# The delta rule's residual of four heads: one broadcast product and one addition in place of four fused operations

## The chip, the cores and the metric

The kernel runs on one core of a Trainium2 chip. The metric is the device time of one execution in microseconds (us): 2305.68 in the median of three runs, from 2304.61 to 2306.77.

A core has engines that work through queues of their own and wait for each other through semaphores: TensorE (PE in the profile; its weight loads are listed as PEld) multiplies matrices, VectorE (DVE), ScalarE (ACT) and GpSimd (POOL) work on tiles, SyncE (SP) issues the transfers. Each engine takes its queue in order: an instruction that waits holds up everything behind it on that engine. Matrix products are written to PSUM, which has eight banks; all else lies in SBUF.

## The reference

Two layers of a hybrid block: a Mamba-2 branch (SSD), latent attention (MLA) and a gated DeltaNet branch read one input projection; their outputs are gated, projected and followed by an MLP. Sequence 512, width 1024, everything in float32. The change lies in the DeltaNet branch, whose core is this (cut):

```python
    rhs = jnp.concatenate([v * beta[..., None], kb * jnp.exp(g)[..., None]], axis=-1)
    sol = lax.linalg.triangular_solve(a_mat + jnp.eye(L, dtype=jnp.float32), rhs,
                                      left_side=True, lower=True)
    u, w = jnp.split(sol, [DV], axis=-1)
...
    def step(state, inp):
        qc, kc, uc, wc, gc, ac = inp
        v_new = uc - jnp.einsum('bhld,bhdv->bhlv', wc, state)
        o = (jnp.einsum('bhld,bhdv->bhlv', qc * jnp.exp(gc)[..., None], state)
             + jnp.einsum('bhlm,bhmv->bhlv', ac, v_new))
        g_last = gc[..., -1:]
        state = (state * jnp.exp(g_last)[..., None]
                 + jnp.einsum('bhld,bhlv->bhdv', kc * jnp.exp(g_last - gc)[..., None], v_new))
        return state, o
...
    o = rmsnorm(o, norm_g) * jax.nn.silu(z.astype(jnp.float32).reshape(Bsz, S, GDN_V_HEADS, GDN_HEAD_V))
```

There are eight value heads of width 128 and four key heads of width 128, so that two value heads share a key head. The kernel puts the solve behind the state: it forms the residual r = v - decay * (k . state) of a chunk first and multiplies it with the inverse of the triangular matrix, which gives v_new.

## The kernel before

*Dense products.* A projection is made of fp32r products of 128x512. To keep float32's accuracy each weight and each activation is split into a high and a low half, and each product is three matmuls (L182, L183, L184). A weight is loaded by SP (L161, `wraw`, two buffers), cast to its high half on ACT (L154, `whi`) and subtracted on DVE (L155, `wlo`); of `whi` and `wlo` there are four buffers each, so a cast waits until PE has used the half from four casts before. The results go to four PSUM banks called `acc`. Everything else that PE writes goes to three banks `sm`, and transposed outputs to one bank `yt`.

*The DeltaNet part.* `gdn_unit(u, ...)` handles four value heads; it is called for u = 0 and u = 1 in each layer. It first makes queries (`key_tiles`, with norms L968, L970, L972), transposed keys (L977, copied at L978), values (projected and transposed at L988, scaled at L989) and gates. Then it loops over t = 0..3, chunks of 128 tokens:

- L1003 the product of keys and queries, L1005 masks it, L1007 multiplies it into the decays `e` (both its inputs are in SBUF);
- for t > 0: L1012 the product of keys and state into a bank `pk`, then L1014, four fused operations of 128x128, one a head: r = pk * ndec + r. `ndec` is a negative decay, one number for each token and head;
- L1017 multiplies r with the inverse, one product a head; L1019 scales the result to `vn` (tag `wk1`, one buffer), L1024 to `vd` on ACT;
- for t < 3: L1027 the state's update, L1030 (t = 0) or L1033 the new state;
- L1036 and L1041 the two parts of the output, L1042 the copy of the first on ACT (L1046 at t = 0), L1044 adds the second;
- the norm of the output: L1050 squares on ACT with sums, L1056 and L1057 scale the sums, then `rsq`: L258 on DVE and L259, a power, on POOL; L1059 finishes it and L1062 multiplies norm, output and gate, one operation a head.

After the loop L1067 transposes the gated outputs, sixteen of 128x128 in a unit, into `yt`, and L254 and L255 split them into halves. So the norm of chunk t-1 (L1050 to L1062) runs beside the recurrence of chunk t, on the same queues.

*What sets the order.* The program is written in the order above, but the order of each engine's queue comes from a scheduler with priorities, at build time. It fills PE with dense products of other projections: beside u = 0 those for the queries, values and gates of u = 1, beside u = 1 those of the gate inputs and of the output projection. It also pulls single transpositions L1067 up into the loop, and puts casts L154 and splits L155 between the recurrence's work on ACT and DVE. The numbers at the end of tile names below tell buffers apart.

Of the kernel before, what the change touches and what calls it, by code (L numbers as in the profile page):

```python
# [10 lines left out]
F32 = mybir.dt.float32  # L11
# [4 lines left out]
ALU = mybir.AluOpType  # L16
# [4 lines left out]
P = 128  # L21
# [34 lines left out]
def hybrid_kernel(ctx, tc, a, out, depth=2, taps=None):  # L56
    nc = tc.nc
    pe, act, dve, pool, sync = nc.tensor, nc.scalar, nc.vector, nc.gpsimd, nc.sync
    uid = itertools.count()

    def mk(pl, shape, dt, tag, bufs=None):
        return pl.tile(shape, dt, tag=tag, name=f"{tag}_{next(uid)}", bufs=bufs)
# [12 lines left out]
    def bc_last(ap, n):  # L75
        sh = list(ap.shape)
        return ap.unsqueeze(len(sh)).to_broadcast(sh + [n])
# [15 lines left out]
    def sm_bank():  # L93
        return mk(ps_sm, [P, 512], F32, "sm")
# [256 lines left out]
    for ly in range(depth):  # L351
# [198 lines left out]
        for hp in range(4):  # L550
# [121 lines left out]
            if hp == 0:  # L672
                dec, ndec, beta, dtq, dsk = step_sizes()
# [25 lines left out]
        br = bp.enter_context(tc.tile_pool(name="br", bufs=1, reuse_waits="tile"))  # L699
# [102 lines left out]
        hv = lambda x: x.rearrange("p (h n) -> p h n", h=4)  # L802
# [157 lines left out]
        def gdn_unit(u, kT, ork, cc, cd, Yt, yh, yl):  # L960
# [20 lines left out]
            for i in range(2):  # L981
                for j, pj in enumerate(dense_F(weights(w_in, O_GV + (4 * u + 2 * i) * P, 256, D), tiles(256), D, xh, xl)):
                    h = 2 * i + j
# [12 lines left out]
            for t in range(T):  # L996
# [11 lines left out]
                r = v[:, t, :]  # L1008
                if t > 0:
                    pk = sm_bank()  # L1010
                    for i in range(2):
                        pe.matmul(pk[:, i * 256 : (i + 1) * 256], kT[i][:, tok], st[:, i * 256 : (i + 1) * 256], start=True, stop=True)  # L1012
                    for h in range(4):
                        dve.scalar_tensor_tensor(hv(r)[:, h], hv(pk)[:, h], ndec[:, t, 4 * u + h : 4 * u + h + 1], hv(r)[:, h], ALU.mult, ALU.add)  # L1014
                pw = sm_bank()
                for h in range(4):
                    pe.matmul(pw[:, h * P : (h + 1) * P], Y[:, h, :], r[:, h * P : (h + 1) * P], start=True, stop=True)  # L1017
# [77 lines left out]
        for u in range(2):  # L1095
            gdn_unit(u, *mats[u], *yg)
# [97 lines left out]
        with tc.tile_pool(name="wo", bufs=1, reuse_waits="tile") as wo:  # L1194
# [8 lines left out]
            h = mk(hpl, [P, T, D], F32, "h")  # L1203
# [204 lines left out]
```

## Time and profile before

| what | value |
|---|---|
| median of 3 runs | 2305.68 us (2304.61 to 2306.77) |
| the profiled execution | 2304.96 us |
| its span, first to last instruction | 2303.2 us |
| mean clock granted to PE | 0.998 of full speed |
| PE / PEld / DVE / ACT / POOL busy | 98 / 81 / 71 / 52 / 3% of the span |
| window 585 to 664 us (units 0 and part of 1, layer 1) | PE busy 78.10 of 79.00 us, DVE 58.32 |
| window 676 to 714 us (unit 1's loop, layer 1) | PE busy 35.70 of 38.00 us, DVE 24.31 |

All numbers but the first line come from one profiled execution. A row of a group gives line, engine, operation, output and inputs, how many, busy us and mean ns, then the idle time before them and what ended it. A row of the chain of waits gives start, duration and what the end of the program was waiting for at that moment. A row of the timeline gives start, duration, engine, line and operation, and in brackets the idle time before and its releaser. Layer 1's units run at about 585 to 720 us, layer 2's at the same distance from its own start.

### The profile page before, as it was taken

To read this page: it belongs to the slowest core of one execution; us is meant where nothing else is said; L and a number is where in the kernel's file an instruction comes from. 1 tells how busy PE (TensorE), PEld (TensorE's weight loads), DVE (VectorE), ACT (ScalarE), POOL (GpSimd) and SP (SyncE) were. 2 spreads that over 40 slices of the span, in tenths; PEclk is the share of its full clock that TensorE was granted. 3 is DMA by queue.
4 is the path that set the end of the run, shared out by engine and by line. 5 is a ranking of instruction groups with operands and counts; after the bars stand their busy time and mean duration, and the time that the engine had idled before them with its cause. 6 is when DMAs were issued, how large, how long until landed. Compare 5 with 4: busy or idle time off the path is not lost.

```text
span 2303.2 us, 32278 instructions
## 1 busy us (share of the span) xinstructions
PE 2268.3 (98%) x11810; PEld 1864.5 (81%) x11810; DVE 1646.7 (71%) x3256; ACT 1201.6 (52%) x2509; POOL 59.4 (3%) x74
## 2 busy tenths in 40 slices
PE   8999999999999999999999999999999999999998
PEld 7888787888887888888888887878888877888886
DVE  7777566876666778767867775668757667778668
ACT  6766644333443465554657666443334435645545
POOL 0000000000000000000000000000000000000000
PEclk9999999999999999999999999999999999999999
DMA  4223633452324243233132236335422241433231
GB/s 142 80 74 101 192 101 112 130 144 74 87 69 158 71 147 102 92 102 116 49 102 79 74 108 194 97 111 146 120 82 83 65 164 55 156 110 101 92 110 46
DMA packets 220032, 244.16 MB, mean 106 GB/s; under 512 B 34256, under 2 KB 172384, under 8 KB 219872
## 3 DMA queue, kind: packets, MB, share of 16 engines
q1 hardware_dynamic: 219872, 242.09, 34.5%
q8 instruction: 93, 1.52, 0.3%
q14 instruction: 67, 0.55, 0.1%
HBM read 225.60 MB, written 11.74 MB: 103 GB/s over the span
## 4 chain that ended last, share of the span: by engine, by line
PE 91%; DVE 4%; ACT 2%; POOL 1%; DMA 1%; issue 1%; SPq 0%; DVEq 0%; POOLq 0%; ACTq 0%
PE acc L182 23%; PE acc L183 23%; PE acc L184 23%; PE sm L184 3%; PE sm L182 3%; PE sm L183 3%; DVE wlo L155 1%; PE sm L752 1%; PE sm L650 1%; ACT whi L154 1%; PE sm L1036 1%; POOL gms L259 1%; PE yt L666 1%; PE sm L290 1%; PE sm L630 1%
## 5 line engine op out<-in xcount | busy, mean ns | idle before, releaser
L155 DVE TENSOR_TENSOR wlo<-wraw,whi 128x512 fp32r<-128x512 f32 (+1 forms) x536 | 365.8, 687 | 345.1 <-ACT whi L154 338.4
L154 ACT CAST whi<-wraw 128x512 fp32r<-128x512 f32 (+1 forms) x536 | 329.5, 618 | 538.6 <-PE acc L183 366.8
L184 PE MATMUL acc<-xh,wlo 128*128 128x512 f32 (+1 forms) x1344 | 522.8, 389 | 0.0
L182 PE MATMUL acc<-xh,whi 128*128 128x512 f32 (+1 forms) x1344 | 522.7, 389 | 0.0
L183 PE MATMUL acc<-xl,whi 128*128 128x512 f32 (+1 forms) x1344 | 521.7, 388 | 0.0
L183 PEld LDWEIGHTS acc<-xl,whi 128*128 128x128 f32 x1344 | 253.0, 188 | 47.9 <-DVE xl L255 0.7
L182 PEld LDWEIGHTS acc<-xh,whi 128*128 128x128 f32 x1344 | 252.8, 188 | 47.9 <-ACT xh L254 0.4
L184 PEld LDWEIGHTS acc<-xh,wlo 128*128 128x128 f32 x1344 | 252.9, 188 | 47.5
L154 ACT CAST whi<-wr 128x512 fp32r<-128x512 f32 x168 | 104.2, 620 | 108.1 <-PE acc L183 47.8
L183 PE MATMUL acc<-yl,whi 128*128 128x512 f32 x384 | 151.5, 395 | 0.0
L182 PE MATMUL acc<-yh,whi 128*128 128x512 f32 x384 | 150.9, 396 | 0.0
L184 PE MATMUL acc<-yh,wlo 128*128 128x512 f32 x384 | 150.0, 391 | 0.0
L155 DVE TENSOR_TENSOR wlo<-wr,whi 128x512 fp32r<-128x512 f32 x168 | 113.5, 689 | 35.6 <-ACT whi L154 34.8
L691 DVE SCALAR_TENSOR_TENSOR ckl<-acc,pc,ckl 128x511 f32<-128x511 f32 (+2 forms) x168 | 120.4, 744 | 18.1 <-ACT ckl L687 10.8
L182 PEld LDWEIGHTS acc<-yh,whi 128*128 128x128 f32 x384 | 71.7, 188 | 15.9 <-ACT yh L254 1.7
L184 PEld LDWEIGHTS acc<-yh,wlo 128*128 128x128 f32 x384 | 72.2, 188 | 14.5
L183 PEld LDWEIGHTS acc<-yl,whi 128*128 128x128 f32 x384 | 72.2, 188 | 13.8
L183 PE MATMUL acc<-wlo,xh 128*128 128x512 f32 (+1 forms) x208 | 80.1, 385 | 0.0
L182 PE MATMUL acc<-whi,xh 128*128 128x512 f32 (+1 forms) x208 | 79.6, 384 | 0.0
L184 PE MATMUL acc<-whi,xl 128*128 128x512 f32 (+1 forms) x208 | 79.5, 384 | 0.0
L1148 DVE TENSOR_TENSOR h<-h,acc 128x512 f32<-128x512 f32 x120 | 77.1, 682 | 0.1
L454 ACT ACTIVATE eE<-eE,cum 128x128 f32<-128x128 f32 x192 | 63.2, 391 | 25.0 <-DMA eE<-d_c 23.3
(453 smaller groups left out, 4553.3 us busy)
## 6 DMA issues: line engine op xcount, KB each, us to landing
wraw<-in_w_in_dram SPq DMA_DIRECT2D x144, 512.0 KB, 3.7
wraw<-in_w_up_dram SPq DMA_DIRECT2D x64, 512.0 KB, 3.6
wr<-in_w_down_dram SPq DMA_DIRECT2D x32, 1024.0 KB, 5.2
eE<-d_c SPq DMA_DIRECT2D x48, 256.0 KB, 3.9
wraw<-in_w_mla_out_dram SPq DMA_DIRECT2D x16, 512.0 KB, 3.4
eE<-d_e SPq DMA_DIRECT2D x32, 256.0 KB, 2.7
wraw<-in_w_ssd_out_dram SPq DMA_DIRECT2D x16, 512.0 KB, 3.4
wraw<-in_w_gdn_out_dram SPq DMA_DIRECT2D x16, 512.0 KB, 3.3
```

Source lines behind the costliest of these rows:

```text
L154: act.copy(hi, raw)
L155: dve.tensor_tensor(lo, raw, f32(hi), ALU.subtract)
L182: pe.matmul(o, ah, bh, start=start, stop=False, skip_group_check=more)
L183: pe.matmul(o, ah, bl, start=False, stop=False, skip_group_check=more)
L184: pe.matmul(o, al, bh, start=False, stop=stop, skip_group_check=more)
L259: pool.tensor_tensor(o, o, (exp if exp is not None else nhalf)[:, : o.shape[1]], ALU.pow)
L290: pe.transpose(ps[:, j * P : (j + 1) * P], xr[j % 2][:, kk * P : (kk + 1) * P], ident)
L454: act.activation(o[:, i], o[:, i], AF.Relu, scale=-1.0, bias=cum[:, t, h0 + i : h0 + i + 1])
L630: pe.matmul(o, qps[j][:, tok], kps[:, :n], start=False, stop=False)
L650: pe.transpose(ps[:, n : n + P], pn[t][:, kb * P : (kb + 1) * P], ident)
L691: dve.scalar_tensor_tensor(acc[:, d:], ps[:, : S - d], taps_[3 - d], acc[:, d:], ALU.mult, ALU.add)
L1148: dve.tensor_tensor(hs_, hs_, ps[t], op)
```

## The change

The four operations of L1014 become two over all four heads. A new tile `kd_` takes the product of `pk` and `ndec`, where `ndec`'s four numbers a token are spread over 128 columns each by a broadcast access; a second operation adds it to r. `kd_` is of the tag `wk1`, so it takes the one buffer in which `vn` lies.

```diff
                         pe.matmul(pk[:, i * 256 : (i + 1) * 256], kT[i][:, tok], st[:, i * 256 : (i + 1) * 256], start=True, stop=True)
-                    for h in range(4):
-                        dve.scalar_tensor_tensor(hv(r)[:, h], hv(pk)[:, h], ndec[:, t, 4 * u + h : 4 * u + h + 1], hv(r)[:, h], ALU.mult, ALU.add)
+                    kd_ = mk(br, [P, 512], F32, "wk1")
+                    dve.tensor_tensor(hv(kd_), hv(pk), bc_last(ndec[:, t, 4 * u : 4 * u + 4], P), ALU.mult)
+                    dve.tensor_tensor(r, r, kd_, ALU.add)
                 pw = sm_bank()
```

It is one line longer, so what stood at L1017 stands at L1018 in the changed kernel, L1062 at L1063, and so on; the product is L1014 and the addition L1015. It acts at twelve places: two layers, two units, t = 1, 2, 3. 48 operations go and 24 come.

The scheduler makes other queues of it. On DVE at u = 0, t = 1 of layer 1 (`tok_5664` holds r, `tok_5665` the gates and outputs, `gms` the norm, `gk` and `eE` the masked products), from the first operation of the residual on, before:

```order
L1014 SCALAR_TENSOR_TENSOR tok_5664<-sm_6072,ndec_1105,tok_5664 128x128
L1005 TENSOR_TENSOR gk_6069<-sm_6066,ct_75 128x256
L1056 TENSOR_TENSOR gms_6054<-gos_6010,grt_6051 128x4
L1014 SCALAR_TENSOR_TENSOR tok_5664<-sm_6072,ndec_1105,tok_5664 128x128
L1057 TENSOR_TENSOR gms_6054<-gms_6054,grt_6051 128x4
L1007 TENSOR_TENSOR eE_6064<-eE_6064,gk_6069 128x512
L258 TENSOR_SCALAR gms_6054<-gms_6054 128x4
L1014 SCALAR_TENSOR_TENSOR tok_5664<-sm_6072,ndec_1105,tok_5664 128x128
L1059 SCALAR_TENSOR_TENSOR gms_6054<-gms_6054,grt_6051 128x4
L1014 SCALAR_TENSOR_TENSOR tok_5664<-sm_6072,ndec_1105,tok_5664 128x128
L1062 SCALAR_TENSOR_TENSOR tok_5665<-tok_5665,gms_6054,wk_1275_6041 128x128 x3
```

and in the changed kernel:

```order
L1014 TENSOR_TENSOR wk_1286_6075<-sm_6072,ndec_1105 128x512
L1057 TENSOR_TENSOR gms_6054<-gos_6010,grt_6051 128x4
L1005 TENSOR_TENSOR gk_6069<-sm_6066,ct_75 128x256
L1058 TENSOR_TENSOR gms_6054<-gms_6054,grt_6051 128x4
L1015 TENSOR_TENSOR tok_5664<-tok_5664,wk_1286_6075 128x512
L258 TENSOR_SCALAR gms_6054<-gms_6054 128x4
L1007 TENSOR_TENSOR eE_6064<-eE_6064,gk_6069 128x512
L1060 SCALAR_TENSOR_TENSOR gms_6054<-gms_6054,grt_6051 128x4
L1063 SCALAR_TENSOR_TENSOR tok_5665<-tok_5665,gms_6054,wk_1275_6041 128x128 x3
```

The fourth operation of the residual stood behind L1059, which takes POOL's result; now the whole residual stands ahead of L258, which feeds POOL. L1007 stood ahead of L258 and now stands behind it. At t = 2 and 3 the order is alike, with a split L155 behind the product at u = 1.

On PE at the same place, from the third dense product behind L1012 (`xh`, `xl` are halves of the input, `whi`, `wlo` of a weight) to the transposition; before:

```order
L1017 MATMUL sm_6079<-tok_5664,tok_4370 128x128
L183 MATMUL acc_6292<-xl_36_152,whi_6311 128x512
L184 MATMUL acc_6292<-xh_28_144,wlo_6312 128x512
L182 MATMUL acc_6292<-xh_29_145,whi_6311 128x512
L183 MATMUL acc_6292<-xl_37_153,whi_6311 128x512
L1017 MATMUL sm_6079<-tok_5664,tok_4370 128x128
L184 MATMUL acc_6292<-xh_29_145,wlo_6312 128x512
L1017 MATMUL sm_6079<-tok_5664,tok_4370 128x128
L1067 MATMUL yt_6261<-ct_75,tok_5665 128x128
```

and in the changed kernel:

```order
L183 MATMUL acc_6289<-xl_36_152,whi_6308 128x512
L184 MATMUL acc_6289<-xh_28_144,wlo_6309 128x512
L182 MATMUL acc_6289<-xh_29_145,whi_6308 128x512
L183 MATMUL acc_6289<-xl_37_153,whi_6308 128x512
L1018 MATMUL sm_6078<-tok_5664,tok_4370 128x128 x4
L184 MATMUL acc_6289<-xh_29_145,wlo_6309 128x512
L1068 MATMUL yt_6258<-ct_75,tok_5665 128x128
```

The four products with the inverse were spread between the dense ones, a head each; now they stand together, since all heads' residuals come at once. One dense product stands between the last of them and the transposition. How the counts of dense products (L182 to L184) changed at the other places of a layer, up to the product named:

| place | before | in the changed kernel |
|---|---|---|
| u0 t1, L1012 to the transposition, then to the state's update | 10, 11 | 10, 11 |
| u0 t2, L1012 to the state's update | 50: 8 among the four L1017, 7 up to the single L1067, then 35 with the other two L1017 among them | 41: 12 up to the four L1018, 28 up to the single L1068, 1 |
| u0 t3, L1012 to the output L1036 / L1037 | 50 | 23: 15 and 8 |
| u1 t1 | as u0 t1 | as u0 t1 |
| u1 t2, L1012 to the state's update | 26 | 24: 12, 1 up to L1068, 11 |
| u1 t3, L1012 to L1036 / L1037 | 19 | 21: 12, 1 up to L1068, 8 |

On ACT at the end of u0's loop (`whi_66..` are cast weights; `wk_1325` and `wk_1328` the output of t = 3), before:

```order
L154 CAST whi_6610<-wraw_6608 128x512
L154 CAST whi_6626<-wraw_6608 128x512
L154 CAST whi_6644<-wraw_6642 128x512
L1042 COPY wk_1325_6231<-sm_6226 128x512
L262 ACTIVATE ft_1376_6478<-ckl_1377_6479 128x512
L262 ACTIVATE ft_1379_6492<-ckl_1380_6493 128x512
L1050 ACTIVATE gk_6240,gos_6010<-wk_1325_6231 128x128
```

and in the changed kernel:

```order
L154 CAST whi_6557<-wraw_6539 128x512
L687 ACTIVATE ckl_1383_6490<-acc_6406,pc_121 128x512
L262 ACTIVATE ft_1379_6475<-ckl_1380_6476 128x512
L154 CAST whi_6607<-wraw_6605 128x512
L262 ACTIVATE ft_1382_6489<-ckl_1383_6490 128x512
L154 CAST whi_6623<-wraw_6605 128x512
L1043 COPY wk_1328_6228<-sm_6223 128x512
L978 COPY kt_6389<-sm_6391 128x512
```

The copy of the output stands one cast further up in the row of weights (two casts of the next pair ahead of it, where there were three), while its product L1037 moved 27 dense products further up. On PE behind that L1037 there now stand L1042, L968, 8 dense products, a single L1068, 14 dense products, L977, 2, L977, L988, 2, L988, 9 and the first L1068 of t = 3. No other queue changes but SP's, where the load of one chunk's `e` (L1000, u1 t3) stands ahead of two weight loads.

## The prediction

> **What bounds the kernel now.** I read the summary of engines and the chain of waits first, because they say which engine a saved microsecond must come from.
>
> ```profile
> span 2303.2 us, 32278 instructions
> PE 2268.3 (98%) x11810; PEld 1864.5 (81%) x11810; DVE 1646.7 (71%) x3256; ACT 1201.6 (52%) x2509; POOL 59.4 (3%) x74
> PE 91%; DVE 4%; ACT 2%; POOL 1%; DMA 1%; issue 1%; SPq 0%; DVEq 0%; POOLq 0%; ACTq 0%
> ```
>
> TensorE (PE) is busy 98% of the span, and 91% of the chain is PE. VectorE (DVE), whose instructions the change swaps, carries 4% of it. A shorter DVE helps only where PE stands still for it. So the second view is that of line L1014, the four operations to be replaced, with who waited for them; then the chain of waits around the first of its places, u = 0, t = 1 of layer 1.
>
> ```profile
> L1014 DVE SCALAR_TENSOR_TENSOR tok<-sm,ndec,tok x48: 342/347/354, 597.7 to 1844.9; 128x128 f32<-128x128 f32 x48
>   PEld sm L1017: 9.0, 22
> ...
> 590.38 0.89 PE sm L1017 x8
> ...
> 597.70 0.35 DVE tok L1014
> 598.05 0.39 DVE gk L1005
> 598.45 0.07 DVE gms L1056
> 598.52 0.26 DVE tok L1014
> 598.78 0.07 DVE gms L1057
> 598.85 0.60 DVE eE L1007
> 599.45 0.09 DVE gms L258
> 599.54 0.07 issue
> 599.61 1.02 POOL gms L259
> 600.65 0.16 DVE gms L1059
> 600.81 0.27 DVE tok L1014
> 601.13 0.49 PE sm L1017 x2
> ```
>
> 48 instructions stand for 12 places, 6 a layer. The waits on them come to 9.0 us in PE's weight loads, but the chain shows that the fourth L1014 is not late because DVE is slow: it stands in DVE's queue behind L1059, and L1059 waits 1.02 us for GpSimd's (POOL's) power L259, which belongs to the norm of the chunk before. PE waits for POOL through L1014. How PE's work goes on there is read in the timeline, together with a second place, u0 t2:
>
> ```profile
> 601.48 0.48 PE L182 MATMUL acc<-xh,whi 128*128 128x512 f32 x1
> 604.09 1.16 PE L1027 MATMUL sm<-wk,kt 128*128 128x256 f32 x4
> 610.02 0.69 DVE L1007 TENSOR_TENSOR eE<-eE,gk 128x512 f32<-128x512 f32 x1
> 610.20 1.38 POOL L259 TENSOR_TENSOR gms<-gms,nhalf 128x4 f32<-128x4 f32 x1 [9.59 <-DVE gms L258]
> 612.75 0.33 PE L1067 MATMUL yt<-ct,tok 128*128 128x128 f32 x1 [0.50 <-DVE tok L1062]
> 612.84 0.48 PE L184 MATMUL acc<-xh,wlo 128*128 128x512 f32 x1
> ```
>
> PE steps through dense products: between 601.48 and 604.09 there are 11, so 0.237 each, the first at about 0.31 and the others 0.23. At 601.13 and at 612.75 it waits. At the second place the one waiting is not L1017 but L1067, the transposition of a finished norm, and again for POOL.
>
> **The change, part by part.** *DVE's own work.* Four operations of 0.26 us from start to start (598.52 to 598.78 in the chain) make 1.04. The changed kernel has two of 128x512: a product of a PSUM tile with broadcast decays, and an addition of two SBUF tiles. Neither is in the trace at this place, but both kinds are elsewhere:
>
> ```profile
> L1019 DVE TENSOR_TENSOR wk<-sm,gcc 128x512 f32<-128x512 f32 x16 | 11.0, 688 | 3.0 <-PE sm L1017 3.0
> L763 DVE TENSOR_TENSOR tok<-tok,wk 128x512 f32<-128x512 f32 x12 | 8.2, 685 | 0.0
> ```
>
> L1019 is a PSUM product with a broadcast factor, L763 an addition within SBUF: 688 and 685 ns, in the chain 0.60 from start to start (L1007, which is as large). So 2 x 0.60 = 1.20 in place of 1.04: DVE issues 0.16 us more at each place, 1.9 us over 12. DVE has 29% of the span free, so by itself this is hidden; uncovered it would cost the whole 1.9.
>
> *The wait moves.* The order of DVE matters more. In the changed kernel the addition (now L1015) stands ahead of L258, the last step before POOL; no part of the residual is left behind the wait for POOL. The product L1018 (before L1017) then finds its residual ready. But the next user of POOL's result is L1063 (before L1062), and a transposition of it, L1068 (before L1067), stands in PE's queue one dense product behind L1018. The stall goes from L1017 to L1068, it doesn't go away.
>
> How late L1068 is I work out from the start P of the product L1014: 0.60 (L1014) + 0.07 (L1057) + 0.39 (L1005) + 0.07 (L1058) + 0.60 (L1015) + 0.16 (L258 and issue, as at 599.45) = 1.89 to POOL's start. POOL is bounded by its own rows:
>
> ```profile
> L259 POOL TENSOR_TENSOR gms<-gms,nhalf x16: 1006/1007/1518, 599.6 to 1852.7; 128x4 f32<-128x4 f32 x16
> 690.40 1.39 POOL gms L259
> ```
>
> It takes 1.01 where L1007 has run before it, and 1.38 where L1007 starts between L258 and POOL's end (610.02 against 610.20; 690.40 is another such place); 1.52 is the most. In the changed order L1007 follows L258 at every place, so I take 1.39 and keep 1.01 and 1.52 for the range. Then 0.02 of issue, L1060 to the end of the first L1063 0.16 + 0.04 + 0.35, 0.05 to L1068, and 0.09 until the next dense product (612.75 to 612.84 at the stalled L1067): 0.71 in all. Together P + 1.89 + 1.39 + 0.71 = P + 4.0, where the dense work resumes.
>
> [...]
>
> Now place by place, in a layer:
> - u0 t1: P = 597.70, dense work resumes at 601.70 where it did at 601.48, with 11 products ahead of L1027 in both: +0.2.
> - u1 t1: the same orders on PE and DVE: +0.2.
> - u0 t2: the stalled L1067 at 612.75 goes, since its successor stands 28 dense products behind L1018 instead of 7 (below). Up to L1027 there are 41 instead of 50.
>
> ```profile
> 607.97 0.58 PE L184 MATMUL acc<-xh,wlo 128*128 128x512 f32 x1
> 621.53 0.67 PE L1027 MATMUL sm<-wk,kt 128*128 128x256 f32 x2
> 688.55 0.04 DVE tok L1014
> 688.82 0.68 DVE wlo L155
> 696.19 0.46 PE L1027 MATMUL sm<-wk,kt 128*128 128x256 f32 x1
> 700.54 0.35 DVE tok L1014
> 706.43 0.61 PE L1036 MATMUL sm<-wk,eE 128*128 128x128 f32 x4
> ```
>
>   From 607.97: 41 products at 0.23, four L1018 0.89 (as the L1017 at 590.38), a transposition 0.1, and 0.1 each for three restarts after fp32 work (the first product takes 0.31) end at 618.8; before, less 9 x 0.23, it was 619.5: -0.7.
> - u0 t3: 23 dense products ahead of L1037 instead of 50, no stall in either: 0.
> - u1 t2: here a split of weights (L155, 0.68) stands between L1014 and L1057. 688.55 + 4.0 + 0.68 = 693.2; 11 products (2.6) later 695.8. Before: 696.19 less two dense products that moved elsewhere, 695.7. +0.1.
> - u1 t3: 700.54 + 4.68 = 705.2, eight products (1.9) give 707.1; before 706.43 plus the two that came back, 706.9. +0.2.
>
> *The tail of u0.* This is the price that I see least well. With fewer dense products ahead of it, t3's L1037 comes 27 dense products earlier, but its copy on ScalarE (L1043) does not:
>
> ```profile
> 637.01 0.62 ACT L154 CAST whi<-wraw 128x512 fp32r<-128x512 f32 x1 [2.24 <-PE acc L183]
> 638.20 1.16 PE L1036 MATMUL sm<-wk,eE 128*128 128x128 f32 x8
> 639.44 0.58 ACT L1042 COPY wk<-sm 128x512 f32<-128x512 f32 x1 [1.81 <-PE sm L1036]
> 641.76 0.64 PE L977 MATMUL sm<-ct,ft 128*128 128x128 f32 x4
> ```
>
> ACT takes its queue in order, and casts of weights (L154) stand ahead of the copy; each waits until PE has used up an older weight buffer, as the row at 637.01 shows. Before, the copy waited for L1036 alone (638.20, then 639.44), and no wait of PE on L1067 followed. In the changed kernel L1037 would start at 638.20 - 27 x 0.23 = 632.0. But the second of the two casts ahead of the copy takes the buffer of a weight that PE uses up 20 dense products later: 632.0, 3.56 for L1037 to the norms of the next keys (638.20 to 641.76), 20 x 0.23, 0.1 for a restart, 640.3. The cast (0.62) ends at 640.9, and the copy (0.58) at 641.6. A second L977 takes over the copied bank, and two L988 wait for copies of L977's (0.58 each) behind it on ACT: I count 0.3 of waits of PE for them, with the last L988 ending at 643.7. Then come on DVE L989 (0.6, 128x512 like L1007), L1057, L1058 and L258 (0.3), on POOL 1.01 (L1007 isn't near), and 0.6 to the end of L1063: 646.3, and L1068 could go. PE has 9 dense products (2.1) ahead of it: 645.8. So 0.3 + 0.5 = 0.8. The bounds are 0 (the casts come early) and 1.6 (the copy one cast and its issue, 0.8, later); I take 1.2, above the count, because PE's wait there delays the release of the next weight buffers. The tail of u1 keeps its order: 0.
>
> Sum per layer: 0.2 + 0.2 - 0.7 + 0 + 0.1 + 0.2 + 1.2 = +1.2. Two layers with the same orders: **+2.4**. The profiled execution took 2304.96 us (its span 2303.2 and 1.8 around it); 2307.4 for such a one. The median of the runs shown, 2305.68, lies 0.72 above it, so the median forecast is **2308.1**, 0.1% up. About 0.2% (4.6 us) is what a measurement of this kernel can tell from no change, so this is a forecast of no change.
>
> **The rivals.**
> 1. *The wait is hidden anyway.* POOL is not lengthened, and the tail of u0 finds other work. For it: PE has dense work at every place, and POOL's 1.01 is its usual price. Against it: no dense product can pass a stalled L1068 in PE's queue. Each of the four places with L1068 loses 0.38 (u0t1, u1t1 -0.2, u1t2 -0.3, u1t3 -0.1), the tail 0: -0.2 - 0.2 - 0.3 - 0.1 - 0.7 = -1.5 a layer, 2305.68 - 3.0 = 2302.7. Still within 0.2%.
> 2. *Slower: the tail of u0 loses one cast and one split more.* Place: L1043 on ACT. If the weights that free the cast buffer come later, the copy is 0.62 + 0.68 = 1.3 later, L1068 follows, and PE, stalled, frees the next buffers later too. It decides from a copy later than about 642.3. Then 2 x (1.2 + 1.3) = 5.0, with POOL at 1.52 another 1.1: 2311 to 2312, middle 2311.5. For it: ACT's idle time before the cast at 637.01 is 2.24, all waiting for PE. Against it: DVE and ACT have slack in the tail.
> 3. *Faster.* All stalls on L1014 and the one at 612.75 go and none comes back: four of about 0.7 and one of 0.67 are 3.4 a layer, 2305.7 - 6.8 = 2299. For it: PE's chain truly runs through L1014. Against it: the same POOL result is needed one dense product later.
> 4. *It doesn't do what it says*: a broadcast product slower than L1014's four. L1019 has the same form at 688 ns, so I give it nothing of its own.
>
> **How the numbers follow.** The forecast (2306.5 to 2310.3) has 0.45, rival 1 0.23, rival 2 0.27 and rival 3 0.05. Faster by over 0.2% is rival 3 alone, 0.05; slower by over 0.2% is rival 2, 0.27; within 0.2% the rest, 0.68. The range reaches down over most of rival 1 (2302.7) to 2302.5, and up over most of rival 2 to 2312.0; outside are rival 3 and the ends.
>
> **What would show it.** In the changed profile: the sum over L1014 and L1015 near 16.5 us as before (24 of 0.69); no wait of PE on L1015 at L1018; waits on L1063 at L1068 of some 0.7 at u0 t1, u1 t1, t2, t3; POOL's L259 at 1.38 rather than 1.01 in the median; no wait at u0 t2; in the tail of u0, the copy L1043 long after its L1037, and a stall at L1068 of 0.5 or more. The prediction is wrong if L1068 does not wait (then rival 1 or 3), or if the casts L154 in u0's tail start over 1 us later against PE's dense work than before (rival 2).

## The result

The changed kernel takes **2312.26 us** in the median of nine runs (2309.93 to 2312.75), the kernel before 2305.37 in nine (2304.53 to 2307.13): a ratio of 1.0029, 95% interval 1.002 to 1.0037. It is slower by 6.9 us. The forecast was 2308.1, up by 2.4, with a range to 2312.0, and 0.68 on no measurable change. The sign of the shift was right, its size was not, and the case that held the most chance was the wrong one.

The profiled execution took 2312.32 us. Its summary, in the same three lines as before:

```profile
span 2310.5 us, 32276 instructions
PE 2271.3 (98%) x11810; PEld 1865.7 (81%) x11810; DVE 1648.2 (71%) x3232; ACT 1202.0 (52%) x2509; POOL 61.3 (3%) x74
PE 89%; DVE 5%; ACT 2%; POOL 1%; DMA 1%; issue 1%; SPq 0%; DVEq 0%; POOLq 0%; ACTq 0%
```

DVE's busy time is up by 1.5 us, near the 0.16 us a place (1.9 in all) of the prediction. DVE's share of the chain is up by a point, from 4% to 5%: PE waits longer for what DVE hands on late. The groups of PE by line (busy us, mean ns, then idle time just before them and what ended most of it) show where. First the kernel before, then the changed one:

```profile
L1017 PE MATMUL sm<-tok,tok 128*128 128x128 f32 x128 | 23.9, 286 | 3.5 <-DVE tok L1014 3.5
L1067 PE MATMUL yt<-ct,tok 128*128 128x128 f32 x64 | 11.9, 278 | 2.9 <-DVE tok L1062 2.9
L988 PE MATMUL sm<-ct,ft 128*128 128x128 f32 x64 | 9.5, 276 | 0.0
```

```profile
L1018 PE MATMUL sm<-tok,tok 128*128 128x128 f32 x128 | 17.3, 278 | 0.0
L1068 PE MATMUL yt<-ct,tok 128*128 128x128 f32 x64 | 12.3, 284 | 8.9 <-DVE tok L1063 8.9
L988 PE MATMUL sm<-ct,ft 128*128 128x128 f32 x64 | 9.9, 277 | 2.0 <-ACT kt L978 2.0
```

The wait for the residual is gone from 3.5 us to nothing. The wait of the transposition went from 2.9 to 8.9: 5.4 of that are the four places a layer that the prediction named, 1.7 the tail of unit 0, and 1.9 the end of unit 1, where the kernel before has 1.9 too. And a wait of 2.0 stands where there was none, at L988, the transposition of the next unit's values. The first two are the trade that the prediction described; the third is not in it at this size: it counted 0.3 us a layer there.

Every kernel of this study issues 11810 instructions on PE, so the same work lies between the 3300th and the 4000th (588.64 to 727.54 us before: the DeltaNet units of layer 1) and between the 9200th and the 9900th (those of layer 2). The time from one to the other is free of what happens elsewhere in an execution:

| stage | before | changed | difference |
|---|---|---|---|
| DeltaNet units, layer 1 | 138.90 us | 141.47 us | +2.57 |
| DeltaNet units, layer 2 | 139.62 us | 142.35 us | +2.73 |
| 1st to 3000th instruction on PE | 530.60 us | 532.23 us | +1.63 |

So 5.3 us of the 7.3 between the two profiled spans are the change's. Another 1.6 lie at 65 us, where both programs are the same. The view by windows (us, busy time of PE, PEld, DVE, ACT and POOL, then PE's granted clock, DMA share and GB/s) shows what it is, the changed kernel first, the kernel before below:

```profile
62.00:64.00 2.00, 0.93 (x7) 0.74 (x8) 1.34 (x5) 0.75 (x3) 0.63 (x1) 1.00 0.47 172
66.00:68.00 2.00, 2.00 (x6) 1.54 (x6) 1.55 (x3) 0.47 (x2) 0.50 (x1) 0.50 0.00 0
```

```profile
62.00:64.00 2.00, 0.90 (x8) 0.62 (x7) 1.22 (x5) 0.87 (x3) 0.75 (x1) 1.00 0.56 209
66.00:68.00 2.00, 2.00 (x11) 1.52 (x10) 2.00 (x4) 1.27 (x4) 0.62 (x1) 1.00 0.00 0
```

Both have PE idle for 1.1 us there (from 61.97 and from 62.09 us). In the changed kernel's execution PE then ran at half clock for 3.41 us (its clock is 0.82 in the window from 64 to 66 us, 0.50 in the one shown and 0.83 from 68 to 70), which costs half of that, 1.7. In the other it did not.

### The profile page after: what moved, and what is told of

It is laid out like the page before. It is cut to its first block, busy times and chain, and to the rows that moved or that the text cites. A ratio compares the mean times of both kernels' runs of the same rounds, so it can differ in the third digit from the quotient of the medians.

```text
span 2310.5 us, 32276 instructions
## 1 busy us (share of the span) xinstructions
PE 2271.3 (98%) x11810; PEld 1865.7 (81%) x11810; DVE 1648.2 (71%) x3232; ACT 1202.0 (52%) x2509; POOL 61.3 (3%) x74
## 3 DMA queue, kind: packets, MB, share of 16 engines
q8 instruction: 93, 1.52, 0.3%
## 4 chain that ended last, share of the span: by engine, by line
PE 89%; DVE 5%; ACT 2%; POOL 1%; DMA 1%; issue 1%; SPq 0%; DVEq 0%; POOLq 0%; ACTq 0%
PE acc L182 23%; PE acc L183 23%; PE acc L184 22%; PE sm L183 3%; PE sm L184 3%; PE sm L182 3%; DVE wlo L155 1%; PE sm L752 1%; ACT whi L154 1%; PE sm L650 1%; POOL gms L259 1%; PE sm L1037 1%; DMA eE<-d_c 1%; PE sm L1028 1%; PE sm L290 1%
## 5 line engine op out<-in xcount | busy, mean ns | idle before, releaser
L155 DVE TENSOR_TENSOR wlo<-wraw,whi 128x512 fp32r<-128x512 f32 (+1 forms) x536 | 365.2, 686 | 351.5 <-ACT whi L154 340.1
L184 PE MATMUL acc<-xh,wlo 128*128 128x512 f32 (+1 forms) x1344 | 522.4, 389 | 0.0
L182 PE MATMUL acc<-xh,whi 128*128 128x512 f32 (+1 forms) x1344 | 522.3, 389 | 0.0
L182 PEld LDWEIGHTS acc<-xh,whi 128*128 128x128 f32 x1344 | 252.9, 188 | 48.7 <-ACT xh L254 0.4
L184 PEld LDWEIGHTS acc<-xh,wlo 128*128 128x128 f32 x1344 | 252.7, 188 | 48.2
L182 PE MATMUL acc<-yh,whi 128*128 128x512 f32 x384 | 150.7, 396 | 0.0
L184 PE MATMUL acc<-yh,wlo 128*128 128x512 f32 x384 | 150.3, 391 | 0.0
L155 DVE TENSOR_TENSOR wlo<-wr,whi 128x512 fp32r<-128x512 f32 x168 | 113.3, 687 | 35.3 <-ACT whi L154 34.4
L691 DVE SCALAR_TENSOR_TENSOR ckl<-acc,pc,ckl 128x511 f32<-128x511 f32 (+1 forms) x168 | 121.1, 744 | 17.6 <-ACT ckl L687 10.3
L182 PEld LDWEIGHTS acc<-yh,whi 128*128 128x128 f32 x384 | 71.7, 188 | 16.1 <-ACT yh L254 1.7
L184 PEld LDWEIGHTS acc<-yh,wlo 128*128 128x128 f32 x384 | 72.2, 188 | 14.7
L182 PE MATMUL acc<-whi,xh 128*128 128x512 f32 (+1 forms) x208 | 80.0, 385 | 0.0
L184 PE MATMUL acc<-whi,xl 128*128 128x512 f32 (+1 forms) x208 | 78.7, 381 | 0.0
```

The source lines that it names most:

```text
L155: dve.tensor_tensor(lo, raw, f32(hi), ALU.subtract)
L182: pe.matmul(o, ah, bh, start=start, stop=False, skip_group_check=more)
L184: pe.matmul(o, al, bh, start=False, stop=stop, skip_group_check=more)
L691: dve.scalar_tensor_tensor(acc[:, d:], ps[:, : S - d], taps_[3 - d], acc[:, d:], ALU.mult, ALU.add)
```

## The experiments

Each run is given by its edit, what was expected of it, what came, and what follows. Medians are compared with the kernel before on the same chip; the last two columns of the table below, the DeltaNet units of both layers against before (138.90 and 139.62), separate the kernels better, since they hold no half-clock stretch. They come from one profiled execution of each kernel. A wait that the text gives for a product of PE is, where no row stands beside it, the time from the start of the product ahead of it less what that step takes elsewhere; the bracket of a row is about 0.16 us shorter.

| run | median, us | before, us | ratio (95% interval) | layer 1 | layer 2 |
|---|---|---|---|---|---|
| the change | 2312.26 | 2305.37 | 1.0029 (1.002 to 1.0037) | +2.57 | +2.73 |
| e1, unit 0 alone | 2309.19 | 2304.25 | 1.0019 (1.001 to 1.0028) | +1.93 | +1.84 |
| e2, unit 1 alone | 2305.85 | 2304.25 | 1.0008 (0.9999 to 1.0017) | +0.73 | +0.83 |
| e3, change, no L1055 | 2308.17 | 2304.25 | 1.0016 (1.0008 to 1.0025) | +1.54 | +1.70 |
| e4, before, no L1054 | 2306.71 | 2304.25 | 1.001 (1.0001 to 1.0019) | +0.33 | +0.29 |
| e5, change, late transposes | 2307.51 | 2304.49 | 1.0013 (1.0004 to 1.0022) | +1.40 | +1.55 |
| e6, change, latest transposes | 2316.53 | 2304.49 | 1.0052 (1.004 to 1.0065) | +6.10 | +5.71 |
| e7, before, late transposes | 2306.06 | 2304.49 | 1.0007 (0.9998 to 1.0016) | +0.63 | +0.58 |
| e8, four operations first | 2309.90 | 2304.49 | 1.0022 (1.0013 to 1.0032) | +2.63 | +2.29 |
| e9, e3 with a later tail | 2305.97 | 2304.54 | 1.0008 (0.9999 to 1.0017) | +0.95 | +1.10 |
| e10, norm's end on POOL | 2303.39 | 2304.54 | 0.9997 (0.9988 to 1.0006) | -0.37 | -0.46 |
| e11, the same, four operations | 2310.47 | 2304.54 | 1.0024 (1.0014 to 1.0034) | +2.55 | +2.53 |
| e12, e10 with later transposes | 2299.68 | 2304.66 | 0.9978 (0.9969 to 0.9987) | -2.53 | -2.57 |

### Which unit loses

```diff
-                    kd_ = mk(br, [P, 512], F32, "wk1")
...
+                    if u == 0:
+                        kd_ = mk(br, [P, 512], F32, "wk1")
...
+                    else:
+                        for h in range(4):
...
```

> The product and the addition at u = 0 alone (6 of 12 places); u = 1 keeps the four operations of L1014. Theory A (the loss is in the tail of u = 0, where on DVE the scaling L1055 waits for POOL's power of the next keys, L972, and holds up L155 and L1045): most of the loss stays, +2.0 us a layer, about 2309.4 (2310.9 if the half-clock stretch at 65 us of the changed profile comes with it). Theory B (the two operations are dearer than the four wherever they stand): half the loss, about 2308.8 with it, each of six places the same. Theory C (the stretch at half clock at 65 us, 1.6 us, has nothing to do with the edit): it may be there or not.

> The product and the addition at u = 1 alone; u = 0 keeps the four operations. Theory A: no tail of u = 0 is changed, what is left is the stall on L1068 and the lengthened POOL, +0.6 us a layer, about 2306.6. Theory B: half the loss, about 2308.8. The median of e1 and e2 taken from before add up to the change's 6.9 us in both; only the split differs.

The orders of the unit with the change are those of the changed kernel, those of the other unit those of the kernel before. The two parts add up: 3.77 and 1.56 us over both layers are 5.33, where the change costs 5.30; per layer they are near the +2.0 and +0.6 that theory A expected. Six places each cost 3.8 and 1.6, so the two operations as such are not what is dear (theory B); unit 0 is. In its trace the places of unit 0 gain 0.7 us a layer, and the stretch behind them, from the output product of t = 3 to the first place of unit 1, loses 2.6. The profile of e1 has its half-clock stretch at 1206 us, layer 2's counterpart of 65 us, that of e2 at 64.5; at 65 us all kernels of this study run the same order on PE, and e1, with the edit in unit 0, lacks the stretch there, so the edit does not decide it (theory C).

### What the tail waits for

The chain of waits of the changed kernel in the tail of unit 0, layer 1 (start, duration, what the end of the program waited for):

```profile
638.59 0.79 DVE tok L1063 x3
639.38 0.09 DVE gss L970
639.47 0.07 issue
639.54 1.65 POOL grq L972
641.18 0.02 issue
641.21 0.04 DVE grt L1055
...
641.45 0.59 DVE wlo L155
642.04 0.27 DVE wk L1045
642.31 0.02 issue
642.33 0.40 ACT gk L1051 x2
642.74 0.48 ACT kt L978
643.22 0.04 issue
643.26 0.67 PE sm L988 x4
...
643.96 0.69 DVE tok L989
...
645.20 1.02 POOL gms L259
...
646.85 0.33 PE yt L1068
```

And four rows of its timeline, with the idle time before the instruction and its releaser in brackets:

```profile
640.02 0.58 ACT L1043 COPY wk<-sm 128x512 f32<-128x512 f32 x1
641.21 0.24 DVE L1055 TENSOR_SCALAR grt<-grq 128x2 f32<-128x2 f32 x2 [1.75 <-POOL grq L972]
643.26 0.66 PE L988 MATMUL sm<-ct,ft 128*128 128x128 f32 x4 [1.00 <-ACT kt L978]
646.85 0.33 PE L1068 MATMUL yt<-ct,tok 128*128 128x128 f32 x1 [0.83 <-DVE tok L1063]
```

The copy L1043 that the prediction worried about ends at 640.60. But L1045, which needs it, starts at 641.96. Ahead of L1045 in DVE's queue stands L1055, a scaling of the next unit's inverse norms that nobody needs before the next unit's first norm, some 40 us later; it waits 1.75 us for POOL's power L972, and L155 and L1045 wait with it. A square L1051 waits for L1045, the second copy L978 stands behind that square on ACT, and PE's L988 waits for the copy. From that L988 the chain goes on through L989, the steps of the norm and POOL's power to L1068: 2.9 us from the end of L988, against nine dense products (2.1 us) that PE has to do meanwhile. In the kernel before L1054 did not stand ahead of L1044 there. (The section on the change says that no queue changes but those it shows and SP's. In this tail DVE's does, in this way, and POOL's, where L972 now runs before the norm of t = 3 and ran behind it.) Without L1055:

```diff
-                rqt = mk(sp, [P, 4], F32, "grt", 2)
-                for j in range(2):
-                    dve.tensor_scalar(rqt.rearrange("p (i j) -> p i j", j=2)[:, :, j], rq[:, :, t], 128.0 ** -0.5, None, ALU.mult)
+                ij = lambda x: x.rearrange("p (i j) -> p i j", j=2)
+                rqt = bc_last(rq[:, :, t], 2)
...
-                rsq(ms, ms, 1.0 / 128, EPS)
-                dve.scalar_tensor_tensor(ms, ms, 0.5, rqt, ALU.mult, ALU.mult)
+                rsq(ms, ms, 1.0 / 128 / 128, EPS)
+                dve.scalar_tensor_tensor(ij(ms), ij(ms), 0.5 * 128.0 ** -0.5, rqt, ALU.mult, ALU.mult)
```

> The changed kernel without L1055: the inverse norms of the queries are read by broadcast from POOL's result, their constant goes into the scales of the two operations that follow. Orders stay alike but for L1055. Theory A: in the tail of u = 0 the first L1045 starts 1.2 us earlier, the wait of about 1 us at the second L988 goes, L1068 of t = 3 still waits some 0.7; -1.2 us a layer or a little more, so about 2.4 to 3 us under the changed kernel: 2309.5. My prediction's reading (the copy L1043 stands behind casts): the copy is as late as before and so is all behind it, 2312.

> The same removal of L1054 in the kernel before (control). All theories: its order has no wait behind L1054 in the tail, so no change, 2305.4 within 0.5.

e3 takes 1.03 us off each layer of the change (1.2 expected), and its trace has the second L988 0.1 us late at most; what is left is the transposition:

```profile
639.89 0.62 PE L988 MATMUL sm<-ct,ft 128*128 128x128 f32 x4
643.49 0.33 PE L1067 MATMUL yt<-ct,tok 128*128 128x128 f32 x1 [0.93 <-DVE tok L1062]
```

So the wait at L988 was L1055's, as expected, and not the casts' ahead of the copy: in e3 L1045 starts 0.15 us behind the copy and PE waits no more than 0.1 for what follows from it. The control missed: the same removal costs the kernel before 0.3 us a layer (its median, 2.5 us up, is the profiled execution, which has a half-clock stretch at 10.6 us). Against that the removal is worth 1.3 in the changed kernel.

The remaining wait was taken apart by moving the transpositions of t = 3 on:

```diff
-                    pe.transpose(ps[:, t * P : (t + 1) * P], gz[:, t, c * P : (c + 1) * P], ident)
+                    with tc.high_priority(-200) if t == 3 and u == 0 else nullcontext():
+                        pe.transpose(ps[:, t * P : (t + 1) * P], gz[:, t, c * P : (c + 1) * P], ident)
```

> The changed kernel without L1055, as in the run without the scaled copy, and with the transpositions of t = 3 at u = 0 given 200 places less priority. All orders are those of that run but for the tail of u = 0, where the first transposition of t = 3 stands 19 dense products behind the values' transpositions instead of 9. Theory A: the wait of 1.09 us at that transposition was for the norm alone and 10 dense products (2.3 us) cover it: 1.0 us a layer less than that run, so about 2 us less, near 2306 where that run had 2308. Rival (the tail waits for something else, as a release of weight buffers that comes as late): no change against that run.

It gave 0.59 and 0.60 us a layer against e3, not 1.0 (the medians, 2.2 apart, come from two chips). The wait at the first transposition of t = 3 is gone, but later ones and a dense product behind them wait some 0.5 that they did not wait before. The kernel stays 1 us a layer above the one before, with no wait left in the tail of unit 0 that is larger than 0.35. What this last microsecond is made of stays open: in layer 1 0.84 of it lies in the stretch of the tail, which has 36 more dense products than before.

### What the loops wait for

If L1068 in the loops only stood too early, moving it away would be a gain.

```diff
-                    pe.transpose(ps[:, t * P : (t + 1) * P], gz[:, t, c * P : (c + 1) * P], ident)
+                    with tc.high_priority(-100):
+                        pe.transpose(ps[:, t * P : (t + 1) * P], gz[:, t, c * P : (c + 1) * P], ident)
```

> The changed kernel with the transpositions L1068 given 100 places less priority; the single ones that stood one dense product behind L1018 now stand behind the next chunk's first products. Theory A (at t = 1 to 3 the changed kernel loses only because L1068 waits for POOL's power): in the loops neither L1018 nor L1068 waits; against the kernel before each of the four places with a stalled L1017 gains 0.4 to 0.65 us, u0 t2 0.75, u0 t3 0.2; the tail of u0 still loses 1 to 2.6. In sum -1 to -2.5 us a layer against before, so 2 to 5 us under it. Rival (PE's wait has its cause in the recurrence itself, and comes out at the next product, L1028, instead): the same time as the changed kernel without its tail, about 0 against before.

> The same with 300 places less priority: all transpositions of u = 0 stand in u = 1's first chunks, those of u = 1 behind its loop, and none stands in the tail of u = 0 before the values' transpositions. Theory A: the loops gain as in the run with 100 places, and the tail of u = 0 loses at most the wait at L988 (1.2 us, behind L1055), not the one at L1068 (1.0): -2 to -3.5 us a layer against before, 4 to 7 us under it, unless the output projection waits for u = 1's late halves (then up to 2 us a layer less). Rival: about 0.

> The kernel before, with its four operations of L1014, and the transpositions L1067 given 100 places less priority. Theory A: the last L1014 still stands behind L1059 and POOL, so L1017 waits as before (0.65 at four places a layer); only the stalled L1067 of u0 t2 goes: 0 to -1 us a layer. Rival (all waits come from the transpositions): as much gain as with the changed arithmetic.

Theory A fell in this form; the rival of e5 was right on the place, not on the time (about 0 against before, and 1.4 and 1.55 a layer were measured). L1068 no longer waits in the loops, but L1028, the state's update, does, at u0 t1, u1 t1 and u1 t2, and L1037 at u1 t3. The chain of waits of e5 at u0 t1 names the way:

```profile
602.12 0.26 DVE tok L1063
602.38 0.60 DVE wlo L155
602.99 0.26 DVE tok L1063
603.25 0.61 DVE wk L1020
...
604.21 0.37 ACT wk L1025
604.58 0.04 issue
604.62 0.70 PE sm L1028 x2
```

L1020 scales the product L1018, which ended at 601.0. It starts at 603.2, because on DVE it stands behind the L1063 of the chunk before, and these behind L1060, which waits for POOL (its row has 0.90 us of idle time before it). The wait of DVE for POOL is the constant (0.87 us at L1059 before, 0.90 at L1060 in the changed kernel and 0.90 in e5, all at u0 t1); which product of PE pays for it depends on what stands behind it. In the kernel before that is L1014, so L1017 waits; in the changed one L1063, so L1068 waits; in e5 L1020, so L1028 waits.

e6 missed by far: with the transpositions of unit 1 behind its loop, PE's dense products of the output projection wait for the halves that ACT and DVE make of them, four waits of 0.94 us in layer 1, and there are more at L988, L1028 and L1037. That the single bank `yt` is the reason was not tested.

```profile
718.97 0.70 ACT yh L254
719.67 0.04 issue
719.72 0.77 PE acc L182 x2
```

e7 removes the stalled L1067 of u0 t2 (-0.71 there) and keeps the four waits at L1017 (0.64 to 0.71 in its trace); it loses more than that elsewhere, 0.6 a layer worse in all, where 0 to -1 was expected.

The other question is whether two operations or four matter at all, once their place is the same. Four operations, all ahead of the norm:

```diff
-                    for h in range(4):
-                        dve.scalar_tensor_tensor(hv(r)[:, h], hv(pk)[:, h], ndec[:, t, 4 * u + h : 4 * u + h + 1], hv(r)[:, h], ALU.mult, ALU.add)
+                    with tc.high_priority():
+                        for h in range(4):
+                            dve.scalar_tensor_tensor(hv(r)[:, h], hv(pk)[:, h], ndec[:, t, 4 * u + h : 4 * u + h + 1], hv(r)[:, h], ALU.mult, ALU.add)
```

> The kernel before with its four operations of L1014, given high priority, so that all four stand ahead of the norm on DVE, as the two operations do in the changed kernel. Theory A (the place in DVE's queue matters, not two operations or four): no wait of PE for POOL at L1018's place; the transposition stands behind the next chunk's first products, and the state's update has 7 dense products ahead of it instead of 11, so that up to 0.5 us may be lost there: 0 to -2 us a layer against before. Theory B (the two operations themselves are dear): the four, free of them, gain at every place, -3 us a layer.

From L1012 to the state's update, less 0.2275 us for each dense product, e8 needs 1.9 to 2.0 us at every place; before it was 2.6 to 2.9, and 2.0 at u0 t3. So the four, put first, do remove POOL's wait from that stretch. The time comes back right behind it: with 11 dense products in a chunk the next chunk's L1003 waits 0.9 for its bank, which the copy L1043 has still to empty, and the transpositions at the ends of the two units wait 1.7 and 1.85. It is as slow as the change, where theory A expected 0 to -2 us a layer and theory B -3. Whether two operations or four matter at the same place it does not settle: the scheduler left other dense products beside them (11 at every place, where the change has 21 to 41).

### Taking POOL's wait off DVE

Nothing in the trace asks DVE to finish the norm. The last two steps go to POOL for t < 3; what remains on DVE is a product that waits for no power. Besides this e10 has the removal of L1055 from e3 and the transpositions 100 places later from e5; e11 is the kernel before with the same norm and the same transpositions, its L1054 kept.

```diff
-                dve.scalar_tensor_tensor(ms, ms, 0.5, rqt, ALU.mult, ALU.mult)
-                for h in range(4):
-                    gzh = hv(gz[:, t, :])[:, h]
-                    dve.scalar_tensor_tensor(gzh, gzh, ms[:, h : h + 1], hv(o)[:, h], ALU.mult, ALU.mult)
+                if t < T - 1:
+                    gzt = gz[:, t, :]
+                    dve.scalar_tensor_tensor(gzt, gzt, 0.5 * 128.0 ** -0.5, o, ALU.mult, ALU.mult)
+                    pool.tensor_tensor(ij(ms), ij(ms), rqt, ALU.mult)
+                    pool.tensor_tensor(hv(gzt), hv(gzt), bc_last(ms, P), ALU.mult)
+                else:
...
```

> The changed kernel without L1055; for t < 3 the gate and output are multiplied ahead (128x512, DVE) and the norm is multiplied in on POOL (128x4, then 128x512 with a broadcast factor), so that nothing on DVE waits for POOL in the loops; transpositions 100 places later. Theory A (POOL's wait at the head of DVE's queue is what PE waits for, at L1017, L1067, L1068 or L1028 in turn): in the loops no wait of PE over 0.5 us, -0.3 to -0.7 us at each of u0 t1, u1 t1, u1 t2, u1 t3 and -0.75 at u0 t2 against before; with a tail that loses about 1: -1 to -2 us a layer against before, so 2300 to 2302.5. Rival (the long operations of POOL slow DVE's, as L1007 slows POOL's): the same as before or slower.

> The same norm on POOL and the same later transpositions with the four operations of L1014 (L1054 kept). Theory A: without POOL's wait on DVE, four operations or two make little difference: within 1 us a layer of the run with two, the products L1017 are spread over the dense ones again. Rival (two operations are dearer): 1.9 us or more under the run with two, over 12 places.

In e10 four places behave as expected: against before, -0.66 at u0 t1, -0.74 and -0.68 at u1 t1 and t2, -0.63 at u0 t2. u1 t3 gains nothing (0.3 to 0.7 expected), and u0 t3 loses 1.42. POOL's new steps cost it little:

```profile
L1062 POOL TENSOR_TENSOR gms<-gms,grq x12: 201/202/388, 600.2 to 1842.2; 128x4 f32<-128x4 f32 x12
L1063 POOL TENSOR_TENSOR tok<-tok,gms x12: 1038/1039/1041, 600.5 to 1842.4; 128x512 f32<-128x512 f32 x12
...
  POOL tok L1063: 5.6, 6
```

But transpositions now wait for POOL's product (the last row, from the view of L1074: what PE and its weight loads waited for there, 5.6 us in 6 waits; in layer 1 one of 1.36 at u0 t3), and the first transposition of t = 3 in the tail still waits 1.05 us. The gain is 0.83 over both layers, less than the 1 to 2 a layer expected and too little for the medians to tell. e11 went against both expectations: not within 1 us a layer of e10, but 3 above it. With four operations spread among the other work, the last L1017 comes late: at u0 t1 the 7 dense products ahead of the state's update don't cover L1019 and L1024, and L1027 waits:

```profile
603.18 0.70 PE L1027 MATMUL sm<-wk,kt 128*128 128x256 f32 x2 [1.01 <-ACT wk L1024]
L1027 PE MATMUL sm<-wk,kt 128*128 128x256 f32 x48 | 15.0, 415 | 6.1 <-ACT wk L1024 6.1
```

So in this surrounding the change is worth 5.9 us, in the surrounding it was made for it costs 5.3. Part of that is the order that the scheduler found for each, and e11's L1054; these runs do not separate them from the operations.

The last run moves the two waiting transpositions of e10 on:

```diff
-                    with tc.high_priority(-100):
+                    with tc.high_priority(-200 if u == 0 and t == 3 else -150 if u == 0 else -100):
```

> The run with the norm's end on POOL, with the transpositions of u = 0 later still: 150 places, those of t = 3 200 places (u = 1: 100 as there). In that run PE still waited at two transpositions of u = 0: 1.36 us, in t = 3, for POOL's product, and 1.05 us in the tail, for the norm of t = 3. Theory A: both are covered by dense products now; of the 2.4 us some 0.3 to 0.5 come back in the tail, as in the run with later transpositions of the tail. So about 2 us a layer under that run, 2.4 under the kernel before: 2299 to 2300.5, faster than before by over 0.15%. Rival (what is moved out of the tail comes back as a wait for yt's single bank or for the halves that the output projection reads): no change against that run, 2303.

2299.68 us, ratio 0.9978 (0.9969 to 0.9987), as expected: the one version that beats both kernels. No run has this placement with four operations, or without the norm's end on POOL, so the gain belongs to the edits together. In its loops no product of PE waits for POOL; the groups of PE in its profile, to be held against those of the result:

```profile
L1018 PE MATMUL sm<-tok,tok 128*128 128x128 f32 x128 | 17.8, 282 | 0.4
L1028 PE MATMUL sm<-wk,kt 128*128 128x256 f32 x48 | 14.4, 408 | 0.0
L1074 PE MATMUL yt<-ct,tok 128*128 128x128 f32 x64 | 11.5, 277 | 1.9 <-DVE tok L1068 1.9
```

## Why the prediction was right in its places and wrong in its sum

By its own steps, in layer 1; a place is the time from L1012 to the state's update (t3: to the output product), less 0.2275 us for each dense product between:

| step | predicted | measured |
|---|---|---|
| u0 t1 | +0.2 | +0.27 |
| u1 t1 | +0.2 | +0.28 |
| u0 t2 | -0.7 | -0.75 |
| u0 t3 | 0 | -0.23 |
| u1 t2 | +0.1 | +0.09 |
| u1 t3 | +0.2 | +0.23 |
| tail of u0, and all between the places | +1.2 | +2.68 |
| layer | +1.2 | +2.57 |

**Right: the wait moves.** The chain of waits of the changed kernel at u0 t1 is the sum P + 4.0 of the prediction, step for step:

```profile
599.27 0.69 DVE wk L1014
599.97 0.08 DVE gms L1057
600.05 0.34 DVE gk L1005
600.38 0.07 DVE gms L1058
600.45 0.60 DVE tok L1015
601.06 0.09 DVE gms L258
...
601.22 1.39 POOL gms L259
```

POOL starts 1.95 after the product where 1.89 was predicted, takes 1.39 as predicted, and L1068 starts at 603.24, 3.97 after the product (by the prediction's steps 3.9). L1018 does not wait. **Right: POOL is longer in the new order.** Its median over the sixteen norms is 1.377 us where it was 1.007; it is 1.38 at the twelve with L1007 beside it and 1.01 at the other four. The 1.52 that the prediction kept for its range is another case, a split L155 that runs on for 0.65 us after POOL's start (629.14 us in the kernel before). There, as behind the L1007 that runs on for 0.51 (610.20 us), POOL ends 0.87 after DVE's instruction. No run shows the 1.1 us that rival 2 adds for POOL at 1.52: in the changed kernel no norm's L259 takes more than 1.380. **Right: DVE's own price.** 692 and 685 ns were measured for the two operations, 688 and 685 predicted.

**Wrong: the tail of u0.** The step that failed is the term of +1.2 for the tail, a count of 0.3 us of waits for L977 and L988 and 0.5 for L1068, all put on the copy L1043 behind two casts. The place was right, the term was mis-sized by a wait not seen: the prediction followed ACT's queue and not DVE's, where L1055 stands between L970 and L1045 and waits for POOL's 1.64 us. L988 then waited 1.0 by its row (1.17 against its usual step), and e3 shows that wait to be L1055's. L1068 waited 0.83 (1.00): the way to it from the last L988 took 2.9 us, where the prediction added up 2.5, and that is so without L1055 too. Of the 2.68, 2.59 lie in the stretch from the output product of t = 3 to the first place of unit 1; beside the two waits there are 0.4 in shorter steps, as restarts of dense work (13 where there were 11), with no single wait behind them. Over two layers the line of the tail is 3.1 us dearer than predicted (1.48 in layer 1, 1.64 in layer 2).

The prediction's L1037 was also put too late: it subtracted the 27 dense products of t = 3 and forgot the 9 of t = 2 (2.1 us). The copy stood behind its casts as predicted, 9.1 us after the start of L1037 (8.9 to 9.0 by the prediction's sum), but by e3 it was not in the way.

**Wrong: rival 2's chance.** The second rival named this place and a price (2.5 a layer) that the measured 2.6 to 2.7 comes near, and had 0.27. Its mechanism, later casts and a later copy, is not what happened, so the price was met by luck. Rival 1 (POOL not lengthened) and rival 3 (no stall comes back) fell with the rows above.

**Not foreseeable from one profile: 1.6 us.** 2.4 predicted, 3.1 for the tails and 1.6 for the half-clock stretch make 7.1, where 6.9 was measured. The stretch is in the profiled execution. That most of the other eight runs have it too is argued from their times (seven lie within 0.5 us of the profiled one, one lies 2.4 below) and not shown. The mean clock recorded for each execution fits it (0.999 for the one that lies below, 0.998 or 0.997 for the others), but the half-clock end of an execution (8.15 us in the profiled one, 8.94 in that of the kernel before) moves that digit too.

## What to carry to other kernels

An engine's wait for another engine stands at one point of its queue (here DVE's 0.87 to 0.90 us for POOL), and everything behind it pays; reordering the work around it only changed who paid here. So before splitting or fusing operations around such a wait, look for the instruction that has to wait and ask whether another engine can take it: here the two last steps of a norm on POOL, with the transpositions that read them moved behind enough PE work, gave 5 us, where the reorderings around the wait (e5 to e8) were all no faster than the kernel before. And when a change moves work forward, walk every queue of the stretch it moves into, down to instructions of 0.2 us that belong to something else: what such an instruction waits for counts, not what it takes.

## What was not expected of the hardware

PE ran at half clock for 3.41 us in some executions, always behind one of a few idle spells of the same program: at 65.3 us in the changed kernel, 64.5 in e2, 10.6 in e4, 1206.0 in e1, 1207.8 in e8 and 1207.0 in e9, and not at all before the last 10 us in the other eight profiles. The one at 65.3 us set PE back by 1.63 us against the kernel before, as much as many a change of this size.

In these traces the length of the idle spell did not tell whether half clock followed. In the changed kernel PE was idle for 1.11 us from 61.97 us on, with half clock from 65.3; the same spell in the kernel before, 1.10 us (PE busy 0.90 of the 2 us from 62 to 64), was followed by full clock. In layer 2's counterpart PE was busy for 0.94 of the 2 us from 1202 to 1204 in e1, and its clock was 0.50 from 1206 to 1208; in the kernel before it was busy for 0.85 of the same 2 us, and its clock 1.00. In the changed kernel's own layer 2 it was busy for 0.84 of the 2 us from 1206 to 1208, again with a clock of 1.00 up to 1214. What decides between the two is not shown.
